# An encoder layer on one core: the first eight projection steps written out by hand

## The chip, the cores and the metric

The kernel runs on one core of one Trainium2 chip. A core has a matrix engine (TensorE, PE in the profile), a vector engine (VectorE, DVE), a scalar engine (ScalarE, ACT), GpSimd (POOL) and SyncE (SP), which in this kernel only issues transfers. Each works through its own list of instructions in order; semaphores tie the lists together. The metric is the device time of one execution in microseconds (us), lower is better. Times inside an execution are counted from the start of the profiled span.

## The reference

One pre-norm encoder layer on 1,024 tokens of width 1,024. A projection of the normalised input feeds two attention groups: A, grouped-query attention with RMS-normalised and rotated q and k, and B, neighbourhood attention on a 16 x 64 grid. Each has a SiLU gate; an output projection, a residual and a final RMS norm close the layer.

```python
h = _rmsnorm(x, norm_gain[l])
proj = h @ w_in[l]
q_a, k_a, v_a, g_a, q_b, k_b, v_b, g_b = jnp.split(proj, split_at, axis=-1)
q_a = _rmsnorm(q_a.reshape(b, s, A_HEADS, HEAD_DIM), q_norm_a[l])
k_a = _rmsnorm(k_a.reshape(b, s, A_KV_HEADS, HEAD_DIM), k_norm_a[l])
q_a = q_a * cos + _rotate_half_axial(q_a) * sin
k_a = k_a * cos + _rotate_half_axial(k_a) * sin
o_a = _gqa_blocked(q_a, k_a, v_a) * jax.nn.silu(g_a)
o_b = _neighbourhood_attn(q_b, k_b, v_b, na_rpb[l]) * jax.nn.silu(g_b)
x = x + jnp.concatenate([o_a, o_b], axis=-1) @ w_out[l]
return _rmsnorm(x, final_norm_gain)
```

## The kernel before, in words

**Precision.** Every float32 operand of a matmul is split into a float16 high part and a float16 low part, and three products (high x high, high x low, low x high) are summed. So each input costs a scaling, a copy that rounds to the high part (ACT) and a subtraction that leaves the low part (DVE).

**Tokens and weights.** The tokens are eight x tiles of 128 rows by 1,024. A tile u goes through `load_x` (a DMA into one of four buffers), `x_sq` (sum of squares, L303 on ACT or L305 on DVE), `x_rs` (one tiny DVE operation, L310, and two on POOL, L311 and L312: the row scale), `x_y` (the scaled product on DVE, L315; its float16 copy on ACT, L316; the transpose of that copy into `hT` by DMA, L324) and `x_lo` (the subtraction, L320, and its transpose). The buffer of tile u is free for tile u + 4 once `x_lo(u)` has run. The weights come in groups of 256 columns: group 0 (`KVA`) holds group A's two k heads and two v heads, groups 1 and 2 (`QA`) its eight q heads, groups 3 to 12 the rest, 13 to 16 the output weights. A group is loaded into one of two float32 buffers, its squares are summed (`prep_a`, or in quarters by `squares`, L372), `prep_b` forms a scale (a tiny matmul L388, L390, L391 on POOL), `prep_c` makes the high part (ACT, L397), `prep_d` the low part (DVE, L404), `prep_e` five tiny DVE operations. From group 3 on, `split` does the last two in quarters (L414, L419).

**Steps, chunks and pairs.** A projection generator makes one weight group for one pair of token tiles: 48 matmuls of 128x256 (L504), given out in eight chunks of six. The pair's result lies in one of two PSUM buffers until it has been fetched. The order on PE is always as written: K/V of tiles 0-1 (pair 1), q group 1 of tiles 0-1 (pair 2), K/V 2-3, q 2-3, K/V 4-5, K/V 6-7, q 4-5, q 6-7 (pair 8), then four pairs of q group 2. A `Flow` holds functions that are due at a step and a position ("pre", "mid", "post", "end"); `run(pos)` calls what is due, in the order in which it was entered, and `fill(n)` lets PE's generators go on by n chunks. A pair that ends in step s enters for step s + 1 its fetch out of PSUM (`a`, ACT: L551 and L552, for K/V also V's copy L599), its reduction and inverse root (`b`: L555 and L556 on DVE, the power L557 on POOL) and its rotation (`c`: L561 on DVE, two products L565 on POOL, L568 on DVE, the sum L569 on POOL); and for step s + 2 the high copies (`hi`, ACT: L584 for q; L609 and L610 for k), the subtraction (DVE: L585 or L615) and the transposes (SP: L588; L621 and L623) that give `qTa` and `kTa`. For K/V the low part of V (L603, DVE) is entered for s + 1 at "mid"; it is the last read of that PSUM buffer.

**Who orders what.** PE's instructions are in written order throughout. Within `with tc.manual_schedule(engines={...})` the same holds for the engines named. Elsewhere a planner with a cost model places the instructions of the other engines. Before the change, the hand-ordered block covers only the start (x tiles 0 to 2, weight group 0). The nine steps after it, and the first six units of attention, are the planner's; from unit 6 on (`HAND = 6`) group A's attention is hand-ordered again.

**Attention A.** 64 units, one per q head and token tile. A unit has four score matmuls (L741, L743), for which the first unit needs all of `kTa`; DVE's reduction (L748), ACT's exponential and copy (L750, L751), DVE's subtraction (L756), a transpose (L761), and five units later 24 small matmuls with V (L773 to L775). Beside that each unit lets PE's generators go on by some chunks, fixed by `FILL_A` (5 in the first four units, 4.2 in the next seven) and by `CHUNKS_A`, the total.

## Time and profile before

| | |
|---|---|
| time before, median of 3 runs | 562.96 us |
| lowest and highest | 559.62 and 567.09 us |
| the profiled execution's own time | 561.51 us |
| its span in the trace | 559.7 us |
| PE busy | 515.3 us, 92% |
| DVE busy | 445.9 us, 80% |
| ACT busy | 367.9 us, 66% |
| POOL busy | 151.2 us, 27% |
| first projection matmul | 14.34 us |
| first score matmul of attention A (L741) | 84.92 us |

The profile is one execution. Its page gives the busy time of each engine, the chain of work that ended last, and the costliest groups of instructions; the trace behind it answers with instructions in order of time. A row of the timeline has the start, the duration, the engine, the line, the operation with output and inputs, the shapes and a count; in brackets stands how long the engine was idle before it and what ended that. "PE q" or "SPq" is an engine's queue of issues.

### The profile page before, as it was taken

The numbers are of one execution on the slowest core, as the hardware profiler recorded it, in microseconds if no ns is written. First come the engines' busy times: TensorE is split into PE (matmuls) and PEld (weight loads), VectorE is DVE, ScalarE is ACT, GpSimd is POOL, SyncE is SP. The second block draws the span as 40 slices with busy tenths as digits, with TensorE's granted clock in tenths as the row PEclk, the third lists the DMA queues.
The fourth block names the chain that finished last, engine by engine and source line by source line (L and its number), as shares of the span: only waits on it lengthen the run. The fifth ranks groups of instructions, "written<-read, shape, count | busy, mean of one in ns | idle before, by whom it ended". The sixth has DMA issues, their size and how long they took to land.

```text
span 559.7 us, 13774 instructions
## 1 busy us (share of the span) xinstructions
PE 515.3 (92%) x5583; PEld 402.1 (72%) x5583; DVE 445.9 (80%) x911; ACT 367.9 (66%) x583; POOL 151.2 (27%) x170
## 2 busy tenths in 40 slices
PE   2668989989999999999999999999999987999994
PEld 0456877767887555568888888988777765778883
DVE  4589688889887988778879888677988988988532
ACT  5546466958877768777696786558688768663211
POOL 2395887570000000000000021533622211214100
PEclk9979999998999999999999999999999998999998
DMA  8998738789999999998997989444796999987612
GB/s 245 217 187 234 124 62 208 124 144 191 207 210 206 155 225 189 188 200 169 208 203 168 179 178 217 95 119 112 121 202 119 162 242 202 185 160 168 181 39 75
DMA packets 244512, 95.46 MB, mean 171 GB/s; under 512 B 235489, under 2 KB 236001, under 8 KB 242530
## 3 DMA queue, kind: packets, MB, share of 16 engines
q1 hardware_dynamic: 242434, 81.23, 77.5%
q0 software_dynamic: 1728, 12.58, 7.3%
q10 hardware_dynamic: 288, 0.79, 0.5%
q8 instruction: 43, 0.70, 0.5%
q14 instruction: 19, 0.16, 0.1%
HBM read 29.56 MB, written 4.19 MB: 60 GB/s over the span
## 4 chain that ended last, share of the span: by engine, by line
PE 58%; DVE 7%; issue 4%; DMA 4%; ACT 3%; SPq 1%; POOL 1%; DVEq 0%; POOLq 0%; ACTq 0%
PE pj L504 20%; PE pjb L504 10%; PE kb L504 7%; PE s L743 4%; PE s L741 4%; PE pv L774 3%; PE pv L775 3%; PE pv L773 3%; DMA ar<-ar 2%; DVE ar L852 2%; PE sb L504 2%; DMA x2b<-in_x_dram 1%; ACT rq L854 1%; ACT ar L856 1%; DVE ar L861 1%
## 5 line engine op out<-in xcount | busy, mean ns | idle before, releaser
L504 PEld LDWEIGHTS <-hT 128*128 128x128 f16 x2112 | 204.7, 99 | 57.6 <-issue 15.7
L504 PE MATMUL pj<-whl,hT 128*128 128x256 f16 x1680 | 202.7, 279 | 19.8 <-DMA hT<-ar 7.2
L750 ACT ACTIVATE ar<-s,nm,sm 128x1024 f32<-128x1024 f32 x64 | 76.9, 1202 | 56.6 <-DVE nm L748 56.3
L748 DVE CUSTOM_DVE_ANT_0 ar<-s,sm 128x1024 bf16<-128x1024 f32 x64 | 82.0, 1281 | 33.9 <-PE s L743 33.6
L504 PEld LDWEIGHTS <-ar 128*128 128x128 f16 x768 | 74.5, 99 | 14.9 <-issue 4.5
L756 DVE TENSOR_TENSOR ar<-ar 128x1024 f16<-128x1024 f32 x64 | 79.5, 1242 | 1.4 <-ACT ar L751 1.4
L751 ACT ACTIVATE ar<-ar 128x1024 f16<-128x1024 f32 x64 | 67.6, 1057 | 2.1 <-DVE sum L780 0.3
L504 PE MATMUL pjb<-whl,ar 128*128 128x256 f16 x480 | 58.1, 278 | 2.3 <-DVE x2b L992 1.2
L854 ACT ACTIVATE rq<-ar,nm 128x384 f32<-128x384 f32 (+1 forms) x64 | 34.1, 580 | 33.5 <-DVE nm L852 32.9
L504 PE MATMUL pjb<-whl,hT 128*128 128x256 f16 x432 | 50.2, 273 | 0.0
L504 PE MATMUL kb<-hT,whl 128*128 128x512 f16 x192 | 44.5, 379 | 0.0
L419 DVE SCALAR_TENSOR_TENSOR whl<-raw,sm,whl 128x512 f16<-128x512 f32 x52 | 39.4, 784 | 2.8 <-ACT whl L414 2.8
L774 PE MATMUL pv<-va,ar 128*128 128x64 f16 x384 | 40.6, 195 | 0.0
L773 PE MATMUL pv<-va,ar 128*128 128x65 f16 x384 | 40.5, 194 | 0.0
L775 PE MATMUL pv<-va,ar 128*128 128x65 f16 x384 | 40.4, 193 | 0.0
L773 PEld LDWEIGHTS <-ar 128*128 128x128 f16 x384 | 35.9, 97 | 5.5 <-issue 0.3
L774 PEld LDWEIGHTS <-ar 128*128 128x128 f16 x384 | 35.7, 98 | 5.5 <-issue 0.3
L741 PE MATMUL s<-kTa,rq 128*128 128x512 f16 x128 | 38.2, 380 | 0.5 <-ACT ar L750 0.5
L221 POOL DMA_DIRECT2D raw<-in_w_dram x11 | 6.7, 606 | 112.9 <-ACT ar L751 89.0
L861 DVE SCALAR_TENSOR_TENSOR ar<-rq,ar 128x768 f16<-128x768 f32 (+1 forms) x32 | 30.6, 955 | 7.1 <-ACT ar L856 6.9
L895 POOL TENSOR_TENSOR ar<-ar,qkg 128x256 f32<-128x256 f32 x16 | 18.6, 1161 | 64.4 <-DVE qkg L893 64.4
L775 PEld LDWEIGHTS <-ar 128*128 128x128 f16 x384 | 35.8, 99 | 0.0
(168 smaller groups left out, 941.8 us busy)
## 6 DMA issues: line engine op xcount, KB each, us to landing
raw<-in_w_dram POOLq DMA_DIRECT2D x11, 1024.0 KB, 7.7
ar<-in_x_dram SPq DMA_DIRECT2D x7, 512.0 KB, 6.3
raw<-in_wo_dram SPq DMA_DIRECT2D x3, 1024.0 KB, 6.6
khh<-ar SPq DMA_DIRECT2D x16, 128.0 KB, 3.2
x2b<-in_x_dram SPq DMA_DIRECT2D x4, 512.0 KB, 8.1
x<-in_x_dram SPq DMA_DIRECT2D x4, 512.0 KB, 5.5
out_dram<-x2b SPq DMA_DIRECT2D x8, 256.0 KB, 3.8
out_dram<-x SPq DMA_DIRECT2D x7, 256.0 KB, 2.9
```

What stands on the lines that cost most here:

```text
L419: dve.scalar_tensor_tensor(wp[g][1][:, q], raw[g][:, q], col(S_ + g), wp[g][0][:, q], op0=OP.mult, op1=OP.subtract)
L504: pe.matmul(*o[0], **o[1])
L741: pe.matmul(s[:, c * 512:(c + 1) * 512], q, kTa[:, 4 * c:4 * c + 4, hh], start=True, stop=False)
L748: dve.tensor_tensor_reduce(out=hl[:, 1].bitcast(BF16), in0=s, in1=col(SHA).to_broadcast([P, 1024]), scale=col(NSA), scalar=3e38, op0=OP.ad ...
L750: act.activation(p32, s, AF.Exp, bias=nm, scale=col(SCA))
L751: at(0, "mid", lambda: act.activation(hl[:, 0], p32, AF.Copy))
L756: dve.tensor_tensor(hl[:, 1], p32, hl[:, 0], op=OP.subtract)
L773: pe.matmul(o, pt[:, kt], va[:, kt, hh, v_hi], start=kt == 0, stop=False)
L774: pe.matmul(o[:, :D], pt[:, kt], va[:, kt, hh, v_lo], start=False, stop=False)
L775: pe.matmul(o, pt[:, 8 + kt], va[:, kt, hh, v_hi], start=False, stop=kt == 7)
L854: act.activation(p32[:, e], t[:, e], AF.Exp, bias=nm, scale=-1.0)
L861: dve.scalar_tensor_tensor(hl[:, 1], p32, 2.0 ** 14, hl[:, 0], op0=OP.mult, op1=OP.subtract)
```

## The change

The hand-ordered block now runs on through eight projection steps on ACT, DVE, POOL and SP.

- **Loads.** SP issues x tile 2 ahead of weight group 1, all four quarters of group 1 in one go, and x tile 3 behind them; tiles 4 to 7 each follow the `x_lo` that frees their buffer. `tables_in` moves behind tile 2's first transpose. The tiny POOL copies that held back weight loads (`gate`) are gone. Group 2's load goes from POOL to SP, in step 3; group 3's load stands on POOL after step 6.
- **Start.** `x_lo(1)` moves from POOL to DVE. `prep_b(1)` moves to PE's third chunk of the first pair, and `prep_c(1)`, `prep_d(1)` follow with x tile 3.
- **Steps.** The first pair is step 0. Steps 1 to 7 each run `ahead_of(i)`, "pre", "b", "mid", `amid(i)`, "post", and then one pair on PE. In step 1 tile 4's square sum and `tables()` stand ahead of the fetch of pair 1; `amid(1)` has two table products, tile 4's product and tile 5's square sum. In step 2 the rest of tiles 4 to 6 and tile 7's square sum (now on ACT) stand ahead of the step's entries. In step 3 the rest of tile 7.
- **Group 2's weights.** Squares in quarters in steps 5 and 6, scale during step 6, high and low part in step 7. `PREP` goes, and with it `prep`'s branch for groups below 3.
- **A position "b"** between "pre" and "mid", for the reductions of K/V and of q group 1.
- **Attention** begins after eight pairs instead of nine; `CHUNKS_A` is 272 instead of 264, so the pair is done beside the units.

```diff
-CHUNKS_A = 264
+CHUNKS_A = 272
...
-PREP = {2: 4, 3: 0, 4: 2}
...
         if second:
             second()
+        self.run("b")
         self.run("mid")
...
     load_x(1)
+    load_x(2)
     raw[1] = wraw.tile([P, KC, GC], F32, tag="raw", name="raw1")
...
-    load_w1(*range(2))
+    load_w1(*range(4))
+    load_x(3)
...
     def prep(g):
-        if g < 3:
-            d = PREP.get(g, 1)
-            at(d + 1, "pre", prep_a, g)
-            at(d + 2, "mid", pend.append, g)
-        else:
+        if g > 2:
             want.add(g)
             try_split(g)
...
-        at(1, "post" if g == QA + 1 else "mid", b)
+        at(1, "post" if g == QA + 1 else "b", b)
...
         prep_a(0)
-        load_w1(2, 3)
...
-        load_x(2)
         x_lo(0, dve)
+        load_x(4)
         x_y(1)
-        load_x(3)
+        prep_d(0)
+        x_sq(2, act)
+        x_lo(1, dve)
+        load_x(5)
+        x_rs(2)
         prep_a(1)
-        x_lo(1, pool)
-        prep_d(0)
+        x_y(2)
         tables_in()
-        x_sq(2, act)
-        load_x(4)
-        x_rs(2)
-        load_x(5)
+        x_sq(3, act)
         prep_e(0)
-        x_sq(3, act)
-        x_y(2)
+        k, q = [kva_gen(up) for up in UP], group(1, [qa_gen(0, up) for up in UP])
+        fl.add(k[0], q[0], k[1], q[1], k[2], k[3], q[2], q[3], *group(2, [qa_gen(1, up) for up in UP]))
+        fl.fill(2)
+        prep_b(1)
+        fl.fill(6)
+        fl.slot += 1
+        x_lo(2, dve)
+        load_x(6)
         x_rs(3)
...
+        prep_c(1)
+        x_y(3)
+        prep_d(1)
+        x_lo(3, dve)
+        load_x(7)
+        prep_e(1)
...
+        def ahead_of(s):
+            if s == 1:
+                x_sq(4, act)
+                tables()
+            if s == 2:
+                x_lo(4, dve)
+                x_y(5)
+                x_sq(6, act)
+                x_rs(6)
+                x_lo(5, dve)
+                x_y(6)
+                x_sq(7, act)
+                x_rs(7)
+            if s == 3:
+                x_lo(6, dve)
+                x_y(7)
+                x_lo(7, dve)
+                raw[2] = wraw.tile([P, KC, GC], F32, tag="raw", name="raw2")
+                sp.dma_start(raw[2], w[2])
+                wss[2] = [tn(f"wss2_{i}", 1, "ws") for i in range(4)]
+            if s == 5:
+                q_sq(0, 1)
+            if s == 6:
+                q_sq(2, 3)
+                pend.append(2)
+            if s == 7:
+                alloc_wp(2)
+
+        def amid(s):
+            if s == 1:
+                x_rs(4)
+                for i in (2, 3):
+                    scale_tab(i)
+                x_y(4)
+                x_sq(5, act)
+                x_rs(5)
+            if s == 2:
+                for i in (0, 1):
+                    scale_tab(i)
+
+        for i in range(1, 8):
+            ahead_of(i)
+            fl.run("pre")
+            fl.run("b")
+            fl.run("mid")
+            amid(i)
+            fl.run("post")
+            fl.fill(PAIR)
+            fl.run("end")
+            fl.slot += 1
+            if i == 6:
+                load_w(3)
```

The removed lines not shown are the nine steps' old body: `fl.step(PAIR)`, then the preparation of group 1 and of tiles 3 to 7, the loads of groups 2 and 3, and eight more `fl.step(PAIR)`.

More of the change, by code (lines that the diff above doesn't have):

```diff
@@ L1090 @@
-    prep_e(1)
-    gate[2] = 6
-    scale_tab(1)
-    x_rs(7)
-    x_y(7)
-    load_w(2)
-    gate[3] = 5
-    x_lo(7, dve)
-    load_w(3)
-    for p in range(8):
-        fl.step(PAIR)
+        k, q = [kva_gen(up) for up in UP], group(1, [qa_gen(0, up) for up in UP])
[6 more added lines that the diff above has]
+        load_x(6)
+        x_rs(3)
@@ new lines, with q_sq @@
+        prep_c(1)
[4 more added lines that the diff above has]
+        prep_e(1)
+        def q_sq(*qs):
+            for i in qs:
+                act.activation(va_more.rearrange("p (k c) -> p k c", c=GC), raw[2][:, QUARTERS[i]], AF.Square, accum_out=wss[2][i])
+        def ahead_of(s):
[25 more added lines that the diff above has]
+                alloc_wp(2)
```

28 lines of the change are left out of this document (removed).

## The prediction

> **What bounds the kernel now.** I read the page first, its span and the chain that ended last.
>
> ```profile
> span 559.7 us, 13774 instructions
> ...
> PE 58%; DVE 7%; issue 4%; DMA 4%; ACT 3%; SPq 1%; POOL 1%; DVEq 0%; POOLq 0%; ACTq 0%
> ```
>
> The chain is mostly TensorE, but an average over stages decides nothing. So next came the busy times by stretch, cut at the start-up, the projection steps, the first attention units and the steady part of group A's attention. After the length stand busy time and count of PE, its weight loads, DVE, ACT and POOL, then the granted clock, the DMA share and GB/s.
>
> ```profile
> 10.00:40.00 30.00, 16.72 (x95) 11.73 (x95) 22.06 (x52) 17.77 (x25) 17.54 (x18) 0.89 1.05 224
> 40.00:85.00 45.00, 39.93 (x347) 33.88 (x346) 37.05 (x70) 24.58 (x48) 34.25 (x40) 0.96 0.63 142
> 85.00:137.00 52.00, 48.80 (x491) 38.73 (x490) 46.62 (x72) 38.56 (x59) 29.09 (x22) 0.97 0.87 162
> 137.00:370.00 233.00, 233.00 (x2772) 174.34 (x2771) 190.41 (x334) 171.55 (x228) 23.57 (x36) 1.00 0.97 187
> ```
>
> From 137 to 370 PE is busy for 233 of 233 us, so a delay of PE ahead of that is handed on to the end whole. PE alone, in order of time, for the stretch that the change rewrites (and one row of the chain of waits for the pace at full clock):
>
> ```profile
> 14.34 1.89 PE L504 MATMUL pj<-whl,hT 128*128 128x256 f16 x8 [2.91 <-DMA hT<-ar]
> ...
> 31.99 4.61 PE L504 MATMUL pj<-whl,hT 128*128 128x256 f16 x20 [5.87 <-ACT whl L397]
> ...
> 84.92 0.59 PE L741 MATMUL s<-kTa,rq 128*128 128x512 f16 x2
> ...
> 133.81 2.62 PE pj L504 x24
> ```
>
> 24 matmuls take 2.62 us, a pair of token tiles (48) 5.24. Before the first score matmul (L741, 84.92) nine pairs have run, 47.2 us of work in the 70.6 us since 14.34. So 23.4 us are lost in waits and half clock; that is what the change can win.
>
> **The balance of the change.** It runs eight pairs instead of nine ahead of attention and gives the ninth (eight chunks) to the attention units. PE has no free time there, so nothing hides it: +5.24. If the first score matmul then starts at Q, the time moves by (Q - 84.92) + 5.24. A gain needs Q under 79.7.
>
> Q follows from the four hand-ordered queues. That such a queue is strict shows in the part of the prologue that is hand-ordered already: tile 2's product was done on DVE at 22.0, but its ACT copy (L316) waited until 24.11 behind tile 3's square sum (L303), which waited for its DMA.
>
> ```profile
> 12.31 1.22 DVE L320 TENSOR_TENSOR ar<-ar 128x1024 f16<-128x1024 f32 x1
> ...
> 15.44 2.34 DVE L404 SCALAR_TENSOR_TENSOR whl<-raw,sm,whl 128x2048 f16<-128x2048 f32 x1
> ...
> 20.72 1.28 DVE L315 SCALAR_TENSOR_TENSOR ar<-ar,xs,gain_p 128x1024 f32<-128x1024 f32 x1
> ...
> 23.06 1.06 ACT L303 ACTIVATE ar<-ar 128x1024 bf16<-128x1024 f32 x1 [3.46 <-DMA ar<-in_x_dram]
> ...
> 24.11 1.04 ACT L316 ACTIVATE ar<-ar 128x1024 f16<-128x1024 f32 x1
> 24.47 0.56 POOL L311 TENSOR_TENSOR xs<-xs,mh 128x1 f32<-128x1 f32 x1 [3.79 <-DVE xs L310]
> ...
> 37.68 1.27 POOL L292 TENSOR_TENSOR tabs<-tabs,qkg 128x512 f32<-128x512 f32 x1
> ```
>
> **To 30.9.** DVE's order is unchanged up to prep_d(0), which ends at 17.8 (15.44 + 2.34). Then follow three x_lo at 1.22 (tile 1's comes over from POOL), two x_y products at 1.28, the two halves of prep_d(1) (2.34 as one), two prep_e of five tiny operations (an estimate of 1.0 each) and two trips to POOL for x_rs (0.9 each by estimate: L311, 0.56, and a short operation on either side): 3.7 + 2.6 + 2.3 + 2.0 + 1.8, plus cross-engine gaps of 0.7, is 13.1. ACT keeps up (tile 3's square sum ends near 23.6, and prep_c(1) is ready for prep_d(1)).
>
> Tiles 2 and 3 now go ahead of the first transpose on SP:
>
> ```profile
> ar<-in_x_dram SPq DMA_DIRECT2D x7, 512.0 KB, 6.3
> ```
>
> At the 224 GB/s of 10:40 two tiles take 4.7 us, so the first transpose lands up to 4.7 later than 14.34, or no later if the queue had air. I take 3. It costs nothing: the first projection's output isn't fetched before 33.6 (next step). The same cover hides group 1's weights, which really come sooner: the 5.87 us before 31.99 go, and PE ends its second pair near 32. What is late next is what counts.
>
> **30.9 to 40.8 (step 1).** tables() is about 17 small operations, 2.7 by estimate, to 33.6. Then the first pair's reduction (L555, 0.41, and a small one) and V split, 1.1 by estimate, to 34.7; this also frees its PSUM buffer. x_rs(4) on POOL stands behind the norm's power (rows below, 1.12): to 36.3. Tile 4's product to 37.6, its copy (1.04) and tile 5's square sum (1.06, 0.2 more for the readout by estimate) on ACT, for which DVE waits at x_rs(5): 40.0. Two rotation products of 0.42: 40.8.
>
> **40.8 to 52.5 (step 2).** Here "x tiles ahead of rotations" bites. x_lo(4) and tile 5's product 2.5; copy and tile 6's square sum 2.3; x_rs(6) 0.15; x_lo(5) and tile 6's product 2.5; copy and tile 7's square sum 2.3: 50.5. Only then may ACT make the first K's copies (0.8) and fetch the second pair (L551, L552, 1.1): 52.5. Both projection buffers in PSUM are full until then; PE, done with the third pair near 40, stands for 12 us. Behind DVE's waits at x_rs stand the reductions of both pairs; behind ACT's, every later fetch. SP keeps the same order, and each tile's transposes still land before the pair that reads them (tiles 4 and 5 by 51 for a pair at 64, 6 and 7 by 66 for one at 69). Tile 7's square sum moves from DVE to ACT, where this step counts it.
>
> **52.5 to Q.** From here each step is a rotation. One of K/V and one of Q in the trace of before (its order is the scheduler's):
>
> ```profile
> 68.32 0.36 ACT L599 ACTIVATE va<-pj 128x256 f16<-128x256 f32 x1
> 68.84 0.39 ACT L552 ACTIVATE ar<-pj 128x256 f32<-128x256 f32 x1
> 69.67 0.41 DVE L555 TENSOR_REDUCE nt<-ar 128x4 f32<-128x256 f32 x1
> 70.96 1.12 POOL L557 TENSOR_TENSOR nt<-nt,mh 128x4 f32<-128x4 f32 x1 [0.67 <-DVE nt L556]
> 71.75 0.60 ACT L551 ACTIVATE ar<-pj 128x512 f32<-128x512 f32 x1 [1.22 <-PE pj L504]
> 72.11 0.42 DVE L561 TENSOR_TENSOR ar<-ar,nt 128x256 f32<-128x256 f32 x1 [0.44 <-POOL nt L557]
> 72.67 1.05 POOL L565 TENSOR_TENSOR ar<-ar,tabs 128x128 f32<-128x128 f32 x2 [0.60 <-DVE ar L561]
> 72.91 0.68 DVE L555 TENSOR_REDUCE nt<-ar 128x8 f32<-128x512 f32 x1
> 73.80 0.72 POOL L569 TENSOR_TENSOR ar<-ar 128x256 f32<-128x256 f32 x1
> 74.48 1.64 POOL L557 TENSOR_TENSOR nt<-nt,mh 128x8 f32<-128x8 f32 x1
> 74.56 0.42 ACT L609 ACTIVATE ar<-ar 128x256 f16<-128x256 f32 x1 [1.73 <-POOL ar L569]
> 75.37 0.76 DVE L615 TENSOR_TENSOR ar<-ar 128x256 f16<-128x256 f32 x2 [0.84 <-ACT ar L610]
> 76.16 0.69 DVE L561 TENSOR_TENSOR ar<-ar,nt 128x512 f32<-128x512 f32 x1
> 76.69 2.19 ACT L397 ACTIVATE whl<-raw,sm 128x1024 f16<-128x1024 f32 x2 [1.41 <-POOL sm L391]
> 77.00 2.84 POOL L565 TENSOR_TENSOR ar<-ar,tabs 128x256 f32<-128x256 f32 x2 [0.34 <-DVE sm L436]
> 79.91 2.27 POOL L569 TENSOR_TENSOR ar<-ar 128x512 f32<-128x512 f32 x1
> 82.21 0.63 ACT L584 ACTIVATE ar<-ar 128x512 f16<-128x512 f32 x1
> 86.52 1.90 POOL L565 TENSOR_TENSOR ar<-ar,tabs 128x256 f32<-128x256 f32 x2 [0.27 <-DVE ar L561]
> 88.50 1.27 POOL L569 TENSOR_TENSOR ar<-ar 128x512 f32<-128x512 f32 x1
> ```
>
> The scheduler put Q's fetch (L551, 71.75) ahead of the older K's copy (L609, 74.56), which was waiting for POOL. The new code empties each list in the order in which it was filled, and the older pair's entry is first: copy, then fetch. So step i's fetch waits for step i-1's last POOL sum (L569), and the steps form one loop: copy, fetch, L555, L556, L557, L561, L565, L569. With K/V as the pair fetched: 0.63 + 0.9 (68.32 to 69.23) + 0.41 + 0.2 (L556, an estimate) + 1.12 + 0.42 + 1.05 + 0.72, some 5.6 with gaps. With Q: 0.8 (two of L609) + 1.1 (two of L551, which overlap a little) + 0.68 + 0.2 + 1.64 + 0.69 + 1.9 + 1.27, 8.4 with gaps. PE needs 5.24.
>
> Step 2 from 52.5: L555 to L557 2.5, two table products (L292) 2.5, L565 and L569 3.2, gaps 0.2: L569 ends at 60.9. Steps 3 to 6 fetch K/V, Q, K/V, K/V: 60.9 + 5.6 + 8.4 + 5.6 + 5.8 is 87.3. In step 7 ACT makes the last K's copies (0.8), group 2's weights (L397, 2.19), and fetches Q (1.1); DVE reduces Q (0.9) before it subtracts the K (L615, 0.76): 93.2. Its transpose lands 2.7 after its issue:
>
> ```profile
> kTa<-ar SPq DMA_TRANSPOSE x3, 2.7
> ```
>
> Q is near 96; PE ends its eight pairs at 90 and waits. I take 96.5 for a dozen semaphore hops. Bounds for POOL's two operations in a Q rotation: 1.90 and 1.27 in the one from 86.52, 2.84 and 2.27 in the one from 77.00. DVE mostly waits in this loop, so I take the lower; the upper adds 1.9 to each of the two Q rotations on the path (steps 2 and 4) and, at the same ratios, 1 to each of three K/V: Q at 103. "SBUF — State Buffer" of the Trainium skill ("SBUF: two separate sides") calls the port pair shared by VectorE and GpSimd an exclusive lock held for a whole instruction; taken at its word in every step it speaks for the upper end.
>
> **Half clock.** PE waits some 6 us ahead of Q:
>
> ```profile
> 32.00:37.00 5.00, 4.68 (x21) 0.50 0.97 196
> ```
>
> After the 5.87 us wait the clock stayed at 0.50 for at least these 5 us, of which half is lost: 2.5. Between that and nothing (a wait too short) I take 2, as a wait of 6 us is nearest to this one. The Trainium skill's "TensorE: Matmul & The Clock Gate" (Part 1) has about 3.4 us at half rate after an idle window, which would be 1.7 by estimate.
>
> The edits left cost nothing: the gates' tiny POOL copies go, weight 2 comes on SP from about 62 and is wanted at 69 to 75, weight 3 follows step 6. Weight 3's squares and split, done before 85 in before, now fall among the first units: 0 to 4 us more, as DVE has 5.4 us free of 52 in 85:137; I take 0.
>
> **Sum.** (96.5 - 84.9) + 5.2 + 2 is 18.8. On the profiled execution's 561.5 (span 559.7) that is 580. The median, 562.96, lies 1.4 above and inside the runs' spread (559.62 to 567.09). Own range: 573 (Q at 95.5, no half clock, and the 4 us that PE loses in 85:137 regained) to 591 (Q at 103, 2.5, and 3 to 4 for weight 3).
>
> **Rivals.**
> - *Faster: the queues flow.* If the x tiles don't hold up the second pair's fetch, the bound is DVE's load: 22.1 + 37.1 us in 10:85, less about 3 for what moves on, is 56. From 10 without a gap to 66, 70 with the last K's transpose: 70 - 84.9 + 5.2, 552. It decides if the second pair is fetched before 35. For it: the 23.4 lost us; against: the strict queue at 24.11. Chance 0.12.
> - *Neutral: only the x tiles cost.* The fetch comes at 52.5, but rotations then keep PE's pace: five pairs to 78.7, Q at 80, 80 - 84.9 + 5.2 + 2, 564. For it: before made Q's fetch wait for no copy; against: the fill order of the lists. Chance 0.20.
> - *Worse: weight 3 is late.* At unit 6 its projection begins; squares come due at unit 3, and forced work stops PE for 5 to 10 us: 585 to 590 and over. For it: 46.6 of 52 us of DVE; against: four units of time. Chance 0.10.
>
> My forecast has 0.58. The range 562 to 592 holds it, most of the neutral rival and half of the worse one, 8 in 10; it leaves out the faster. About 2% is what a measurement here can tell from no change (552 to 574). Slower by more: the forecast nearly whole and the late weight, 0.65; within: the neutral rival and half the faster one, 0.28; faster: the other half, 0.07.
>
> **What would show it.** Right: first L741 near 96; a PE wait of 10 us or more for ACT L552 near 40 to 52; L315 of tile 7 after 55; ACT's L584 and L609 waiting for POOL L569 in every step; a last PE wait for the transposed K. Wrong: the second pair's L551 before 45, L741 before 90, or a steady part that isn't all PE.

## The result, and the profile after

The changed kernel takes 588.04 us (median of four runs, 585.80 to 590.16), the kernel before 564.39 us beside it (four runs, 559.62 to 567.09): a ratio of 1.050, 95% interval 1.045 to 1.055. It is slower. The forecast was 580 with a range of 562 to 592. The profiled execution took 585.80 us, 24.3 more than the one before. Some kernels below also have a slower state in a few of their runs; a median is over all runs, a ratio leaves those out.

Line numbers shift by two: what were L741, L552, L603 and L569 are L739, L550, L601 and L567 now, weight quarters' low parts L419 are L421. In the experiments that add a line they are one higher still.

The page of the changed kernel, span and chain:

```profile
span 583.9 us, 13782 instructions
...
PE 54%; DVE 13%; ACT 10%; issue 8%; DMA 7%; POOL 6%; SPq 1%; POOLq 0%; DVEq 0%; ACTq 0%
```

PE's share of the chain fell from 58 to 54%, DVE's rose from 7 to 13%, ACT's from 3 to 10%. Busy times by stretch, columns as in the prediction (length, then PE, its weight loads, DVE, ACT, POOL, granted clock, DMA share, GB/s):

```profile
10.00:40.00 30.00, 18.41 (x138) 14.28 (x138) 22.00 (x52) 17.45 (x24) 9.39 (x15) 1.00 1.09 229
40.00:85.00 45.00, 26.33 (x206) 21.33 (x203) 22.68 (x38) 15.63 (x36) 24.84 (x27) 0.81 0.44 93
96.60:151.40 54.80, 46.08 (x437) 35.94 (x438) 48.00 (x74) 37.48 (x55) 32.36 (x27) 0.91 0.69 140
160.00:382.00 222.00, 222.00 (x2618) 165.00 (x2616) 179.27 (x311) 167.93 (x229) 15.97 (x29) 1.00 1.03 190
```

The start is a little better (18.41 us of PE work in 10:40 where there were 16.72). In 40:85 PE works 26.33 us where it worked 39.93, and no other engine is full: it is a stretch of waits. In 160:382 PE is busy all the time again. PE in order of time, waits in brackets:

```profile
18.95 2.74 PE L502 MATMUL pj<-whl,hT 128*128 128x256 f16 x12 [7.55 <-DMA hT<-ar]
...
51.55 7.32 PE L502 MATMUL pj<-whl,hT 128*128 128x256 f16 x48 [10.50 <-ACT ar L550]
64.98 12.67 PE L502 MATMUL pj<-whl,hT 128*128 128x256 f16 x96 [6.11 <-DVE va L601]
...
91.21 0.38 PE L739 MATMUL s<-kTa,rq 128*128 128x512 f16 x1
...
96.62 0.61 PE L739 MATMUL s<-kTa,rq 128*128 128x512 f16 x1 [5.03 <-DMA kTa<-ar]
...
102.13 0.59 PE L739 MATMUL s<-kTa,rq 128*128 128x512 f16 x2
...
132.12 2.14 PE L502 MATMUL pj<-whl,hT 128*128 128x256 f16 x18 [2.23 <-DVE whl L421]
139.45 1.23 PE L502 MATMUL pj<-whl,hT 128*128 128x256 f16 x5 [5.19 <-DVE whl L421]
...
151.41 0.59 PE L739 MATMUL s<-kTa,rq 128*128 128x512 f16 x2
...
371.07 0.59 PE L739 MATMUL s<-kTa,rq 128*128 128x512 f16 x2
```

The very first score matmul runs at 91.21, on the part of `kTa` that has landed; the second, at 96.62, has waited 5.03 us for the last K's transpose. Q stands for this second one here, and in every experiment whose row shows a wait for `kTa`: from there on attention can go on. The other rows are the start of unit 1 (102.13), of unit 10 (151.41) and of the last unit, 63 (371.07). In the kernel before, units 1, 10 and 63 begin here, and the row below has the busy times of its units 0 to 9:

```profile
89.05 0.59 PE L741 MATMUL s<-kTa,rq 128*128 128x512 f16 x2
...
132.04 0.59 PE L741 MATMUL s<-kTa,rq 128*128 128x512 f16 x2
...
346.33 0.59 PE L741 MATMUL s<-kTa,rq 128*128 128x512 f16 x2
```

```profile
84.90:132.00 47.10, 43.90 (x436) 34.92 (x435) 41.72 (x63) 35.12 (x56) 29.19 (x22) 0.96 0.85 156
```

So the span's 24.2 us (583.9 - 559.7) are made of four parts:

| part | before | after | change |
|---|---|---|---|
| to the score matmul that needs the last K (Q) | 84.92 | 96.62 | +11.7 |
| units 0 to 9 | 47.12 | 54.79 | +7.7 |
| units 10 to 62 | 214.29 | 219.66 | +5.4 |
| from unit 63 to the end | 213.4 | 212.8 | -0.5 |

The third part is the size of the ninth pair, whose eight chunks moved into the units. The first and the second are what the experiments are about.

### The profile page after: what moved, and what is told of

It is laid out like the page before. It is cut to its first block, busy times and chain, and to the rows that moved or that the text cites. A ratio compares the mean times of both kernels' runs of the same rounds, so it can differ in the third digit from the quotient of the medians.

```text
span 583.9 us, 13782 instructions
## 1 busy us (share of the span) xinstructions
PE 515.2 (88%) x5586; PEld 401.7 (69%) x5586; DVE 442.3 (76%) x910; ACT 369.3 (63%) x591; POOL 142.1 (24%) x166
## 4 chain that ended last, share of the span: by engine, by line
PE 54%; DVE 13%; ACT 10%; issue 8%; DMA 7%; POOL 6%; SPq 1%; POOLq 0%; DVEq 0%; ACTq 0%
PE pj L502 20%; PE kb L502 7%; PE pjb L502 7%; PE s L739 4%; PE s L741 4%; DMA raw<-in_w_dram 3%; PE pv L772 3%; PE pv L773 3%; PE pv L771 3%; ACT rq L852 2%; DVE ar L850 2%; PE sb L502 2%; ACT ar L854 2%; DMA x2b<-in_x_dram 1%; POOL nt L555 1%
## 5 line engine op out<-in xcount | busy, mean ns | idle before, releaser
L502 PEld LDWEIGHTS <-hT 128*128 128x128 f16 x2112 | 204.9, 100 | 75.3 <-issue 24.3
L502 PE MATMUL pj<-whl,hT 128*128 128x256 f16 x1680 | 203.2, 280 | 37.2 <-ACT ar L550 10.5
L748 ACT ACTIVATE ar<-s,nm,sm 128x1024 f32<-128x1024 f32 x64 | 76.8, 1200 | 61.5 <-DVE nm L746 61.3
L502 PEld LDWEIGHTS <-ar 128*128 128x128 f16 x768 | 73.6, 98 | 15.8 <-issue 4.5
L502 PE MATMUL pjb<-whl,ar 128*128 128x256 f16 x480 | 56.4, 273 | 4.0 <-DVE x2b L990 3.0
L739 PE MATMUL s<-kTa,rq 128*128 128x512 f16 x128 | 38.9, 384 | 6.3 <-DMA kTa<-ar 5.0
L421 DVE SCALAR_TENSOR_TENSOR whl<-raw,sm,whl 128x512 f16<-128x512 f32 x52 | 39.1, 781 | 2.8 <-ACT whl L416 2.8
L393 POOL TENSOR_TENSOR sm<-wss,mh 128x1 f32<-128x1 f32 x17 | 9.9, 580 | 127.0 <-DVE wss L392 127.0
L771 PEld LDWEIGHTS <-ar 128*128 128x128 f16 x384 | 35.6, 96 | 5.3
L772 PEld LDWEIGHTS <-ar 128*128 128x128 f16 x384 | 35.3, 97 | 5.3
L416 ACT ACTIVATE whl<-raw,sm 128x512 f16<-128x512 f32 x52 | 33.9, 710 | 4.1 <-POOL sm L393 4.0
L773 PEld LDWEIGHTS <-ar 128*128 128x128 f16 x384 | 35.4, 98 | 0.0
```

Source lines behind the costliest of these rows:

```text
L416: act.activation(wp[g][0][:, q], raw[g][:, q], AF.Copy, scale=col(S_ + g))
L421: dve.scalar_tensor_tensor(wp[g][1][:, q], raw[g][:, q], col(S_ + g), wp[g][0][:, q], op0=OP.mult, op1=OP.subtract)
L502: pe.matmul(*o[0], **o[1])
L739: pe.matmul(s[:, c * 512:(c + 1) * 512], q, kTa[:, 4 * c:4 * c + 4, hh], start=True, stop=False)
L748: act.activation(p32, s, AF.Exp, bias=nm, scale=col(SCA))
L771: pe.matmul(o, pt[:, kt], va[:, kt, hh, v_hi], start=kt == 0, stop=False)
```

## Experiments: where the steps' time went

**The order inside step 2.** In the changed kernel step 2 puts x tiles 4 to 7 ahead of the second pair's fetch. Here step 2's "pre" goes ahead of the tiles.

```diff
         for i in range(1, 8):
+            if i == 2:
+                fl.run("pre")
             ahead_of(i)
```

> The changed kernel with one thing altered: in step 2 the entries for ACT (the first K's copies and the fetch of pair 2) stand ahead of x tiles 5 to 7 instead of behind them. Theory (the rotation loop paces, and its start is where DVE is done with the x tiles): PE's 10.5 us wait near 41 to 51 goes, but V's low part of pair 3 comes where it came, PE waits there instead, the first score matmul moves by 1.5 to 2.5 us only, the time falls by 1 to 3. Rival (PE's long wait is lost time): first score matmul 7 to 10 us sooner, time 576 to 579.

Measured: 585.09 us, ratio 1.043 (1.039 to 1.048). PE's waits in that kernel:

```profile
44.16 8.28 PE L502 MATMUL pj<-whl,hT 128*128 128x256 f16 x48 [3.33 <-ACT ar L550]
65.12 13.28 PE L502 MATMUL pj<-whl,hT 128*128 128x256 f16 x96 [12.69 <-DVE va L601]
...
96.69 0.61 PE L739 MATMUL s<-kTa,rq 128*128 128x512 f16 x1 [4.99 <-DMA kTa<-ar]
```

The 10.50 us became 3.33, and the next wait, for the third pair's V behind the same tiles on DVE, grew from 6.11 to 12.69. Q stays (96.69). The theory held, and even the 1.5 to 2.5 us that it allowed for Q did not come. The wait was moved, not removed: the projection has two PSUM buffers, and each of them has to pass the x tiles somewhere.

**The fetch ahead of the older pair.** A list of its own for each pair's fetch and for V's low part, ahead of the older pair's copies and subtractions. The x tiles stay where the change put them.

```diff
-        at(1, "pre", a)
+        at(1, "a" if g != QA + 1 else "pre", a)
...
-            at(1, "mid", vlo)
+            at(1, "v", vlo)
...
             ahead_of(i)
+            fl.run("a")
             fl.run("pre")
             fl.run("b")
+            fl.run("v")
```

> The changed kernel with one thing altered: in every step the fetch of the newest pair out of PSUM (and V's low part) stands ahead of the older pair's copies and subtractions; the x tiles stay ahead of both in step 2. Theory (a loop through copy, fetch and POOL's last sum paces steps 3 to 7): the 10 us wait of PE near 41 to 51 stays, the waits for V's low part at 59 to 65 and at 79 and 86 go, the first score matmul comes near 86 instead of 96.6, and the time falls by 9 to 12 us, to 574 to 577. Rival (only the x tiles of step 2 cost): first score matmul within 2 us of 96.6, time unchanged.

Measured: 577.37 us, ratio 1.030 (1.022 to 1.037). PE's waits:

```profile
51.40 7.05 PE L503 MATMUL pj<-whl,hT 128*128 128x256 f16 x48 [9.85 <-ACT ar L551]
63.99 15.43 PE L503 MATMUL pj<-whl,hT 128*128 128x256 f16 x120 [5.55 <-ACT ar L551]
...
91.12 0.39 PE L740 MATMUL s<-kTa,rq 128*128 128x512 f16 x1 [3.53 <-DMA kTa<-ar]
```

From 64 on PE does 120 matmuls in one go; in the changed kernel it stopped twice more. The loop "copy, fetch, reduction, power, products, sum" of the prediction is broken up by this edit alone, and Q comes 5.5 us sooner. I had said near 86. Three waits stay: two for the fetch behind the x tiles, and one of 3.53 us for the last K's transpose.

**Fetch, reduction and V's low part also ahead of the x tiles**, from step 2 on, where the list of the first experiment still stood behind them:

```diff
+            if i > 1:
+                fl.run("a")
+                fl.run("b")
+                fl.run("v")
             ahead_of(i)
```

> The changed kernel, hand-ordered, with the fetch, the reduction and V's low part of the newest pair ahead of the x tiles from step 2 on, and ahead of the older pair's copies in every step (both orders that the theory blames undone). Theory: PE's wait near 41 to 51 shrinks to under 5 us, no step waits for POOL's last sum, first score matmul at 78 to 86, the first ten units as long as in the changed kernel (54 us), time 566 to 574. Rival (the x tiles' chain through DVE, ACT and POOL paces either way): first score matmul above 89, time above 576.

Measured: 573.96 us, ratio 1.023 (1.020 to 1.026), Q at 85.98. One wait of 10.2 us for V's low part is left in the steps.

**The planner back in steps 1 to 7**: the loop with the same calls, outside the hand-ordered block.

```diff
-        for i in range(1, 8):
-            ahead_of(i)
+    for i in range(1, 8):
+        ahead_of(i)
...
```

> The changed kernel with one thing altered: steps 1 to 7 stand outside the hand-ordered block, so that the planner may order ACT, DVE, POOL and SP there; the same instructions, loads and weight order. Theory (the written order is what costs): the loop of copy, fetch and POOL's last sum is gone, first score matmul at 80 to 88, time 566 to 576. Rival (the loads, the late weights 2 and 3 or the x tiles' chain cost whatever the order): first score matmul above 93, time above 580.

Measured: 574.11 us, ratio 1.023 (1.020 to 1.026), Q at 85.83. The planner, with the change's own calls, gets what the hand order gets when its two queue faults are mended. Of the 24 us, the order that was written by hand for these steps cost some 14 by the medians (588.04 and 574.11), or 11 by the spans of the two profiles (583.9 and 572.8).

**The loads of tiles 2 and 3 as before.**

```diff
     load_x(1)
-    load_x(2)
...
     load_w1(*range(4))
-    load_x(3)
...
         x_rs(1)
+        load_x(2)
         x_lo(0, dve)
-        load_x(4)
         x_y(1)
+        load_x(3)
+        load_x(4)
```

> The changed kernel with one thing altered: x tiles 2 and 3 are loaded where the kernel before loads them, behind weight group 1 and the first transposes. Theory (the first projection's start is covered by DVE's chain): first projection matmul 3 to 5 us sooner than 18.95, first score matmul within 1 us of 96.6, time unchanged within 2 us; x tile 3's square sum may wait for its load and add up to 1. Rival (the loads ahead of the transposes are part of the loss): 3 to 5 us less.

Measured: 587.52 us, ratio 1.048 (1.041 to 1.055). The first projection matmul comes at 14.48 again instead of 18.95, and Q is no better (97.65). What the loads cost lies under later waits.

**Attention a step sooner, in the kernel before**: eight steps and 272 chunks, nothing else.

```diff
-CHUNKS_A = 264
+CHUNKS_A = 272
...
-    for p in range(8):
+    for p in range(7):
         fl.step(PAIR)
```

> The kernel before with one thing altered: eight steps ahead of attention instead of nine and CHUNKS_A 272, the planner's order kept. Theory (the first units are limited by DVE, which now gets one more rotation there): first score matmul about 5 us sooner, 79 to 81, the ten units behind it longer by 2 to 4 us more than the moved chunks explain, time 0 to 4 us above before. Rival (PE paces, the move is free): time within 1 us of before. Second rival (starting sooner is a gain): 2 us or more below.

Measured: 560.54 us, ratio 1.0003 (0.997 to 1.004). The first rival held: the ninth pair costs the same on either side of Q. Nor did the extra rotation lengthen the first units: in this profile units 0 to 9 took 46.4 us (79.06 to 125.47), where the kernel before needs 47.1. So the +5.4 in the table is no loss of its own: without a better prologue it would only have been set off by a Q that comes 5.2 us sooner.

## Experiments: where the first units' time went

**Weight 3's squares due three units sooner.** PE's two waits of 7.4 us in all at 130 to 139 are for weight 3's low part (L421). In the program its squares come due four steps behind the load, and its sums, scale and split only after them.

```diff
-            squares(g, 4)
+            squares(g, 1 if g == 3 else 4)
```

> The changed kernel with one thing altered: the sums of squares of weight group 3 are due one step after its load instead of four, so that its scale and split can start in units 1 and 2 instead of 4 and 5. Theory (PE's 2.2 and 5.2 us waits for L421 in unit 7 are the price of weight 3's lateness): both waits go, and the half clock behind them; first score matmul at 96.6 as it was; time 6 to 9 us less, 577 to 580. Rival (DVE is simply full in the first units): the wait moves to another DVE operation, time within 2 us.

Measured: 585.22 us, ratio 1.044 (1.039 to 1.049). The squares themselves did not move: the planner runs them at 95 to 98 us in both kernels. What came sooner is the rest: the sums on PE, whose order is fixed, at 109.37 instead of 118.03, and the first low part at 119.1 instead of 131.3. The waits for L421 are gone. PE's waits in the units:

```profile
120.28 0.59 PE L739 MATMUL s<-kTa,rq 128*128 128x512 f16 x2 [1.06 <-ACT ar L748]
125.89 0.59 PE L739 MATMUL s<-kTa,rq 128*128 128x512 f16 x2 [1.24 <-ACT ar L748]
...
148.17 0.59 PE L739 MATMUL s<-kTa,rq 128*128 128x512 f16 x2 [3.53 <-ACT ar L748]
```

They are for the exponential (L748) now, which stands behind DVE's reduction of the scores. Units 0 to 9 take 51.3 us instead of 54.8, units 10 to 62 give back 3.4 (223.1 for 219.7), and the span ends 0.4 sooner than the changed kernel's. My theory, that the lateness of these low parts is the whole cause, fell; most of the wait only moved.

**Fewer chunks in the first units**, 3.8 and 3.4 instead of 5.0 and 4.2, the rest spread over the later ones.

```diff
-FILL_A = [(4, 5.0), (7, 4.2)]
+FILL_A = [(4, 3.8), (7, 3.4)]
```

> The changed kernel with one thing altered: 3.8 and 3.4 chunks a unit in the first four and the next seven units of attention A instead of 5.0 and 4.2; the total stays 272, so later units take more. Theory (DVE is the limit of the first ten units, 48 us of work in 54.8): rotations come further apart, PE's waits there (1.3, 2.2, 5.2 us and the half clock behind them) go for the most part, first score matmul at 96.6, time 4 to 8 us less, 578 to 582. Rival (waits in the first units don't matter for the end): within 2 us of the changed kernel.

Measured: 587.12 us, ratio 1.046 (1.043 to 1.050). My expectation failed, the rival held. Of the waits for L421 5.5 us stay, and the chunks left out must be done later, when PE is full: units 0 to 9 take 47.5 us, 7.3 less, and units 10 to 62 take 226.3, 6.7 more.

**Weight 3 by hand, sooner.** Load in step 4, squares in steps 6 and 7, sums and scale ahead of unit 0, split entered in unit 0. In the changed kernel only the load stands in the steps (after step 6); squares, sums and split are the units' jobs.

```diff
     def prep(g):
-        if g > 2:
+        if g > 3:
...
+            if s == 4:
+                raw[3] = wraw.tile([P, KC, GC], F32, tag="raw", name="raw3")
+                sp.dma_start(raw[3], w[3])
...
+            if s == 6:
+                q_sq(0, 1, g=3)
+            if s == 7:
+                q_sq(2, 3, g=3)
...
-            if i == 6:
-                load_w(3)
+        prep_b(3)
+        at(0, "pre", alloc_wp, 3)
+        at(0, "pre", prep_c, 3)
+        at(0, "post", prep_d, 3)
+        at(8, "pre", load_w, 5)
```

> The changed kernel, with weight 3 loaded in step 4, squared in steps 6 and 7, and scaled and split by hand in unit 0, so that its four eighth-size ACT copies, its four low parts on DVE and its sums are no longer jobs of units 2 to 9. Theory A (weight 3's preparation inside the units is what makes them long): both waits of PE for the low part of weight 3 are gone, units 0 to 9 take 48 to 50 us instead of 54.8, and the median falls from 588 to 581 to 584. Theory B (the units are long because VectorE has one rotation more to do and falls behind, and weight 3 is only where it shows): the wait moves to another instruction, units 0 to 9 stay within 2 us of 54.8, and the median stays at 586 to 588.

Measured: 597.11 us, ratio 1.061 (1.053 to 1.069): 9 us slower than the changed kernel. And yet units 0 to 9 took 48.3 us, as theory A said. Units 12 and 13, counted from 0, took 25.1 us (a pair of usual ones 8.4); these are the "14 to 15" of the next expectation, where 18.8 is the length of one, not the excess. SP's transposes, PE's wait, the weight loads (median us to landing) and the busy times of that stretch, four views of this run:

```profile
147.13 10.92 SPq L759 DMA_TRANSPOSE ar<-ar  x1
158.16 9.51 SPq L644 DMA_TRANSPOSE qTb<-ar  x1
167.77 6.81 SPq L759 DMA_TRANSPOSE ar<-ar  x1
```

```profile
173.99 0.24 PE L771 MATMUL pv<-va,ar 128*128 128x65 f16 x1 [11.90 <-DMA ar<-ar]
```

```profile
raw<-in_w_dram POOLq DMA_DIRECT2D x2, 1024.0 KB, 18.9
```

```profile
162.00:174.00 12.00, 0.10 (x2) 0.02 (x2) 0.09 (x1) 0.14 (x2) 0.00 (x0) 0.66 1.17 100
...
185.00:365.00 180.00, 180.00 (x2064) 129.82 (x2061) 147.88 (x260) 137.06 (x184) 6.69 (x19) 1.00 1.05 191
```

For 12 us almost nothing computes; the transfer engines are as busy as ever (1.17, where the later stretch has 1.05), at 100 GB/s where later there are 191. The two weight loads beside it took 16.6 and 21.2 us (median 18.9); the page of the changed kernel has 7.2 for ten such loads. The first of the two, weight 5's, was issued at 141.0 and landed only at 157.6; it was late before the second was issued at 152.9. As I had put this load at unit 8 by hand, its place was the suspect.

**The same with that load at unit 3.**

```diff
-        at(8, "pre", load_w, 5)
+        at(3, "pre", load_w, 5)
```

> The run with weight 3 by hand (597.11 us), and in it the load of weight 5, which I had put at unit 8, moved to unit 3. There units 0 to 9 had come down from 54.8 to 48.3 us, as theory A said, but units 14 to 15 took 18.8 us more than they should, while PE waited 11.9 us for a transpose and the two weight loads beside it landed after 18.9 us instead of 6.7. If the place of that load made the second stall, it is gone: units 0 to 9 stay at 47 to 50 us and the median falls to 579 to 583, below the 588 of the changed kernel. If the stall belongs to weight 3's new order as such, it stays within 10 us of where it was and the median at 592 to 599.

Measured: 579.66 us, ratio 1.035 (1.030 to 1.040), 8 us better than the changed kernel by the medians, 6 by the spans (583.9 and 577.9). The busy times of its units 0 to 9:

```profile
97.00:145.10 48.10, 44.39 (x433) 34.90 (x434) 44.38 (x68) 34.80 (x51) 32.43 (x25) 0.96 0.78 153
```

48.1 us instead of 54.8. Both stalls are gone, the one for L421 and the new one; three waits for the exponential, 3.6 us in all, stay, and Q stays (97.04). So weight 3's preparation, as the changed kernel had it, cost 6.7 of the 7.7 us. It is not that its work left the units. DVE's 44.38 us instead of 48.00 are one score reduction and one subtraction fewer in the window; the weights' low parts take 3.9 us in it, against 4.2 in the changed kernel. What moved is their time: weight 3's low part runs at 109.6 to 112.1, in units 2 and 3, instead of 131.3 to 139.4, in unit 7, where PE already wants it.

The new stall isn't tied to weight 3's order alone, though. The profiled execution of the experiment with attention a step sooner in the kernel before (568.26 us) has one like it: a load issued at 165.65, 0.35 us behind a transpose, landed after 16.3 us, the transpose after 17.8, and PE waited 4.83 us.

## Experiments: can the parts make a gain

**All at once.** The fetch first, weight 3 by hand (load of weight 5 at unit 8):

> Weight 3 by hand as in the run beside it, together with the fetch, the normalisation and the low part of V put ahead of the x tiles and of the older copies (573.96 us by itself). Theory A: the two gains add, 567 to 570 us, with units 0 to 9 at 46 to 49 us. Theory B: 572 to 574 us. By neither is it as fast as the kernel before (561), because the first score matmul stays near 86 and the eight chunks (5.2 us) are still behind it.

Measured: 583.64 us (575.57 to 590.33), ratio 1.029 (1.018 to 1.040). Units 0 to 9 took 46.5 us, but the second stall was here too (a weight load landed after 24.1 us), so this run tells little of the sum.

**The x tiles' squares first.** In 35 to 58 us each tile's square sum on ACT stands behind the copy of the tile before it. Here, with the fetch first, they run at once in step 1, into the free buffer of weight 2.

```diff
             if s == 2:
                 x_lo(4, dve)
-                x_y(5)
-                x_sq(6, act)
-                x_rs(6)
                 x_lo(5, dve)
                 x_y(6)
-                x_sq(7, act)
-                x_rs(7)
...
             if s == 1:
+                raw[2] = wraw.tile([P, KC, GC], F32, tag="raw", name="raw2")
+                free = raw[2].rearrange("p k c -> p (k c)").bitcast(BF16)
+                for u in (5, 6, 7):
+                    x_sq(u, act, free[:, 1024 * (u - 5):1024 * (u - 4)])
                 x_rs(4)
-                for i in (2, 3):
-                    scale_tab(i)
                 x_y(4)
-                x_sq(5, act)
                 x_rs(5)
+                x_y(5)
+                for i in (2, 3):
+                    scale_tab(i)
+                x_rs(6)
+                x_rs(7)
```

> The changed kernel with the fetch, the normalisation and the low part of V first (573.96 us by itself), and besides it the squares of x tiles 5 to 7 on ScalarE at once in step 1, into a free buffer, where each stood behind the copy of the tile before it. Theory: from 35 to 58 us the x tiles go round a ring of square, mean, power on POOL, product, copy, 5.5 us a tile, and this ring, not any engine's work, holds PE for the 10.2 us at 46 to 56 us; with the squares ahead it turns to 3 to 4 us a tile, PE's wait falls to 2 to 6 us, the first score matmul comes at 78 to 82 instead of 86.0, and the median falls to 566 to 570. Rival: VectorE is full there anyway, the wait moves on, first score matmul at 84 to 86, median 572 to 575.

Measured: 571.55 us, ratio 1.020 (1.015 to 1.025), Q at 83.61. The wait of 10.2 us became two of 3.9 and 2.4, as expected, but Q moved by only 2.4: the last K's transpose (a wait of 4.51) now comes last. It was issued at 77.03, 0.13 us behind weight 3's load of 1 MB on POOL (76.90), and landed 6.5 us later; the next experiment moves that load away. Q and time lie between theory and rival.

**This and weight 3 by hand, weight 5 at unit 3.**

> The squares first and the fetch first as in the run beside it, and weight 3 by hand with the load of weight 5 at unit 3. If both gains are there, first score matmul 78 to 82, units 0 to 9 in 47 to 50 us, and 560 to 565 us, level with the kernel before; if only the ring of the x tiles was in the way, 566 to 570; if the second stall comes back, 575 or more.

Measured: 561.36 us, ratio 1.001 (0.999 to 1.004): level with the kernel before. The profile has Q and units 0 to 9 here:

```profile
80.35 0.59 PE L740 MATMUL s<-kTa,rq 128*128 128x512 f16 x2
...
126.54 0.59 PE L740 MATMUL s<-kTa,rq 128*128 128x512 f16 x2 [1.09 <-ACT ar L749]
```

Q at 80.35 and units of 46.2 us, as the first expectation said. With weight 3 loaded in step 4 the last K's transpose, issued at 77.37, lands after 2.8 us instead of 6.5, PE no longer waits for it, and Q comes 3.3 us sooner than in the last kernel. (The kernel with the fetch first shows the same pair of numbers without and with weight 3 by hand, 6.5 and 2.8.) In these units DVE is busy for 44.19 of 46.19 us, 96%. By the prediction's formula that is (80.35 - 84.92) + 5.24, 0.7, and 0.9 less for the units: no change, as measured.

**The fetch ahead of the squares of tiles 6 and 7**, which in that kernel wait 5.2 and 3.9 us on ACT for their loads. The squares of tiles 6 and 7 and tile 5's product go from step 1 back to step 2, behind the fetch:

```diff
             if s == 2:
+                x_y(5)
+                free = raw[2].rearrange("p k c -> p (k c)").bitcast(BF16)
+                for u in (6, 7):
+                    x_sq(u, act, free[:, 1024 * (u - 5):1024 * (u - 4)])
                 x_lo(4, dve)
+                x_rs(6)
                 x_lo(5, dve)
                 x_y(6)
+                x_rs(7)
```

> The last kernel (561.36 us, level with the kernel before), with one order changed: there the squares of x tiles 6 and 7 stood ahead of the second pair's fetch on ScalarE and waited 5.2 and 3.9 us for their loads, so that the fetch ended at 44.8 and PE waited 3.9 us for it. Here the fetch goes ahead of them. If a fetch behind a waiting copy or square is what costs, PE's wait at 41 to 45 us goes, the first score matmul comes at 76 to 79 instead of 80.3, and the median falls to 556 to 560: a ratio of 0.992 to 0.998. Rival: the low part of V or x tiles 6 and 7 come last instead, first score matmul 79 to 81, 560 to 562 us.

Measured: 560.53 us, ratio 0.9995 (0.997 to 1.002). The rival held: the waits of 3.9 and 2.4 us became one of 8.24 for V's low part, and Q stayed.

```profile
54.28 14.66 PE L503 MATMUL pj<-whl,hT 128*128 128x256 f16 x120 [8.24 <-DVE va L602]
...
80.06 0.59 PE L740 MATMUL s<-kTa,rq 128*128 128x512 f16 x2
```

**One good part of the change alone, in the kernel before**: the sums, the scaling and the low part of weight group 1 by hand in and behind step 0.

```diff
-    fl.step(PAIR)
-    prep_b(1)
-    prep_c(1)
+        fl.fill(2)
+        prep_b(1)
+        fl.fill(6)
+        fl.slot += 1
+        prep_c(1)
+        prep_d(1)
...
-    prep_d(1)
```

> The kernel before, with only one part of the change: the sums, the scaling and the low part of weight group 1 put by hand into and right behind projection step 0, where before they came after it and behind the squares of x tile 3. Theory: the 5.87 us for which PE waits at 26 to 32 us shrinks by 2 to 5 us, the x tiles then take part of it back at 52 to 54 us, and the median falls from 561 to 557 to 560. Rival: the x tiles pace the first nine pairs, PE waits for them instead, and the time stays within 1 us of 561.

Measured: 562.12 us, ratio 1.001 (0.998 to 1.005). In place of the wait of 5.87 us stand four shorter ones for the same weights, 4.3 us in all (1.04, 0.44, 1.06 and 1.77), and PE waits 13.8 us in all for x tiles instead of 7.2. The rival held: the tiles pace the steps.

No version tried beats the kernel before by more than its measurement is uncertain.

## Why the prediction was right, and where it was wrong

One term of the prediction failed: weight 3's squares and split among the first attention units, which it allowed "0 to 4 us more" and took as 0. They were the rest of a loss of 7.7 us in those units, 6.3 us, and are why the two profiled executions lie 24.3 us apart where 18.8 was forecast. What the runs show in its place: PE stood 7.4 us for the late low part of weight 3, and with the preparation placed sooner 6.7 us went away. What follows takes the terms one by one.

**Right: the start of attention.** Predicted 96.5 for Q, measured 96.62 (the very first score matmul ran at 91.21 and saved only its own length). How near the two are is partly luck. The sum 60.9 + 5.6 + 8.4 + 5.6 + 5.8 is 86.3, not the 87.3 that the prediction goes on with; added rightly, it would have given 95.5. The four steps took 27.2 us instead of 25.4, and the slip, with a shorter way from there to Q, made up for it. The mechanism holds, step by step. The way to 30.9: the tables begin on DVE at 30.30. The first projection 3 us late with bounds of 0 and 4.7: it is 4.6 (18.95 - 14.34), and the experiment with the loads put back shows that it costs nothing, as argued. Group 1's wait is gone. Step 2's fetch at 52.5 after a wait of 12: at 51.5 after 10.5. ACT in order of time, with the waits that the prediction named:

```profile
47.82 1.06 ACT L318 ACTIVATE ar<-ar 128x1024 f16<-128x1024 f32 x1 [3.42 <-DVE ar L317]
48.79 1.04 ACT L305 ACTIVATE ar<-ar 128x1024 bf16<-128x1024 f32 x1
...
49.83 0.40 ACT L607 ACTIVATE ar<-ar 128x256 f16<-128x256 f32 x1
...
50.44 0.57 ACT L549 ACTIVATE ar<-pj 128x512 f32<-128x512 f32 x1
50.91 0.58 ACT L550 ACTIVATE ar<-pj 128x512 f32<-128x512 f32 x1
...
60.73 1.06 ACT L318 ACTIVATE ar<-ar 128x1024 f16<-128x1024 f32 x1 [9.23 <-DVE ar L317]
...
67.80 0.42 ACT L607 ACTIVATE ar<-ar 128x256 f16<-128x256 f32 x1 [4.67 <-POOL ar L567]
...
76.40 0.63 ACT L582 ACTIVATE ar<-ar 128x512 f16<-128x512 f32 x1 [3.31 <-POOL ar L567]
...
82.51 0.42 ACT L607 ACTIVATE ar<-ar 128x256 f16<-128x256 f32 x1 [3.30 <-POOL ar L567]
...
88.62 0.42 ACT L607 ACTIVATE ar<-ar 128x256 f16<-128x256 f32 x1 [4.57 <-POOL ar L567]
```

Tile 6's copy and tile 7's square sum, the first K's copies, and only then the fetch (L549, L550). From then on every older copy waits for POOL's last sum, and the steps last 6.4, 8.6, 6.1 and 6.1 us from copy to copy (61.37, where that sum ends in step 2, to 88.6), predicted 5.6, 8.4, 5.6 and 5.8. The two experiments on the lists confirm the mechanism: with the fetch ahead of the older copies PE runs its projections without a stop from 64 on.

**Right: contention on POOL, mostly.** Taken was the lower bound, 1.90 and 1.27 for a Q rotation's product and sum. POOL in steps 2 and 4 of the changed kernel:

```profile
57.30 2.73 POOL L563 TENSOR_TENSOR ar<-ar,tabs 128x256 f32<-128x256 f32 x2
60.11 1.26 POOL L567 TENSOR_TENSOR ar<-ar 128x512 f32<-128x512 f32 x1
...
73.17 1.85 POOL L563 TENSOR_TENSOR ar<-ar,tabs 128x256 f32<-128x256 f32 x2 [0.87 <-ACT va L1074]
75.10 1.27 POOL L567 TENSOR_TENSOR ar<-ar 128x512 f32<-128x512 f32 x1
```

Only one of the four operations, the product of 2.73, was near its upper bound (2.84): there DVE worked beside it, and DVE's own subtraction of an x tile at 57.70 took 1.75 us where the next one took 1.23. The lock that "SBUF — State Buffer" of the Trainium skill describes spoke for Q at 103 if it held in every step. The trace agrees in so far as both engines were slower where they worked side by side; that the lock is the reason no run here shows. In the rest of this loop DVE mostly waits.

**Right: half clock and the ninth pair.** Unit 0 lasts 5.51 us (96.62 to 102.13), 4.13 before: 1.4 for the 2 that I took, although the score matmul at 91.21 was done ahead. By the Trainium skill's "TensorE: Matmul & The Clock Gate" (Part 1) it would have been 1.7; 1.4 agrees with that better than with my 2. The ninth pair: 5.4 for 5.24.

**Wrong: weight 3's squares and split among the first units, "0 to 4 us more; I take 0".** They were the rest of the 7.7 us of units 0 to 9, 6.3 beyond the half clock, outside even the upper end. The reason given for 0 was cover, 5.4 us of free DVE in 52. That reckoned with how much work there is and not with when it comes. The squares were done at 98, the sums on PE came at 118 and the low part at 131 to 139, and PE stood 7.4 us for it. With weight 3 by hand and weight 5's load at unit 3 the low part comes at 110, nearly as much of this work stays in the units, and 6.7 of the 7.7 us are gone. Nor is DVE's free time the measure: here it is busy for 88% of the units, in the kernel that came out level for 96%. The rival "weight 3 is late", which I gave 0.10, named the two stalls (2.23 and 5.19 us, at 130 to 139, and half clock behind them), and its 585 to 590 is where the time fell; it was no alternative to the forecast, it came on top. Its reason was only half right: with the split some 11 us sooner those waits went, and most of the time stayed; with the squares, sums and split sooner still, in the steps and the first units, it went too.

The sum by terms: predicted 11.6 + 5.2 + 2 + 0 = 18.8, measured 11.7 + 5.4 + 1.4 + 6.3 - 0.5 = 24.3.

**The rivals that fell.** "The queues flow" would have needed the second pair's fetch before 35. Even in the runs with the squares first it ended at 38.7 or 44.8, and in no version of the changed kernel did Q fall below 80, 10 us above what that rival needs. "Only the x tiles cost", Q at 80, was not the changed kernel; it is roughly what the mended one does.

**What stays open.** Why the transfers slowed down so much, in both kernels with weight 5's load at unit 8 and in one execution of another. The place of that load decided it in one pair of kernels; in which way, no view shows. Nor is it settled why a split at 119 (the squares due sooner) still left waits for the exponential where one at 110 did not: between these two kernels weight 3's squares, the scale and weight 5's load moved as well.

## What to carry to other kernels

A hand-written order is as good as the head of each queue: before anything goes ahead of a fetch that frees a PSUM buffer, ask what that queue's next entry waits for, and put the fetch ahead of every copy that waits for another engine. Work that leaves a prologue needs a place of its own, ahead of the moment at which its result is wanted; "the engine has 10% free" says nothing of when, and was no cover here. And ask what a moved load will run beside: here a transpose on the critical path. Starting a paced stage sooner wins nothing when the same work is due on the same engine on either side of the line.

## What the runs showed of the hardware

- Transposes and 1 MB loads in flight together were at times far slower than usual: 16.6 to 24.1 us for a load instead of 7, 7 to 11 us between transposes, while the transfer engines showed as fully busy and moved 100 GB/s instead of 191. Moving one load five units earlier ended it (7.3 us a load). A milder form is the last K's transpose, 6.5 us right behind a load and 2.8 without it, in two pairs of kernels.
- A wait of PE costs more than its length. The granted clock (the number behind the five busy times) behind the waits of 5.03 us at 91 to 96 and of 5.19 us at 134 to 139 in the changed kernel:

```profile
96.60:99.60 3.00, 2.98 (x12) 1.66 (x13) 2.20 (x7) 1.68 (x6) 2.26 (x2) 0.50 0.43 105
99.60:102.60 3.00, 3.00 (x26) 2.46 (x25) 2.96 (x6) 2.68 (x4) 1.99 (x2) 0.95 0.59 249
139.40:143.00 3.60, 3.55 (x26) 2.14 (x26) 1.74 (x6) 0.15 (x1) 2.34 (x3) 0.50 1.17 137
```

The first half-clock stretch ends within the second row. The other goes on beyond its row: 143.5 to 144 still has 0.50, 144.5 to 145 has 1.00. Half speed for 3 to nearly 5 us is some 1.5 to 2.4 us on top of each wait, an estimate from these rows.
